# All eight Q/K pairs in one Strassen phase, and a rearranged attention pipeline (one-core decoder trunk)

## Chip, cores and metric

The kernel runs on one core of one Trainium2 chip. The metric is the device time of one execution in microseconds (us). A page of the profile and its trace come from one profiled execution. Engines: PE is the matrix engine, DVE the vector engine, ACT the scalar engine (activations), POOL is GpSimd, SP the engine whose queue starts most transfers.

## The reference, cut to what matters

Two layers on a sequence of 1024 positions with width 1024: first a short gated convolution, then dilated sliding-window attention, each followed by a SwiGLU feed-forward network; RMS norms stand between. All of it is float32. The change lies in the attention layer:

```python
BRANCHES = ((128, 1), (512, 4), (2048, 16))      # (window, dilation)

qkv = (h @ w_qkv).reshape(bsz, seq, 3, N_HEADS, HEAD_DIM)      # 16 heads of 64
q, k, v = qkv[:, :, 0], qkv[:, :, 1], qkv[:, :, 2]
for window, dilation in BRANCHES:
    o, l = dilated_branch(q, k, v, rel_bias, window, dilation)  # softmax over a strided band, and its log-sum
    outs.append(o); lses.append(l)
alpha = jax.nn.softmax(jnp.stack(lses, axis=0), axis=0)
o = jnp.sum(alpha[..., None] * jnp.stack(outs, axis=0), axis=0)
return o.reshape(bsz, seq, D_MODEL).astype(h.dtype) @ w_out
```

The kernel merges the three branches: one set of logits a head, one maximum, one sum.

## The kernel before

**Splitting.** Every float32 operand of a large product is split into a high part (rounded, written by ACT, line 145) and a low part (the rest, written by DVE, line 146), and a product is three matmuls: high by high, high by low, low by high. A weight that was loaded raw (line 159) is split a few products ahead of its use.

**Strassen units.** Most large products go through Winograd's form of Strassen: seven products instead of eight (class `Strassen`; its matmuls are lines 571 to 573, each of the seven takes four k blocks of three). `QueryKey` does this for the queries and keys of head pairs: a unit is one pair, its four output blocks are scaled, split and stored to DRAM (`emit`) a step at a time between later products. `QK_PAIRS` is the number of pairs it covers, seven of eight.

**Plain products.** `product` (lines 373 to 375) multiplies without Strassen. `projections` does pair 7 that way, inside attention. `value_tiles` makes the values of four heads at a time (lines 1517 to 1519, 256 wide), written to DRAM in `vdram`; the first such group is made before the first head.

**Attention slots.** The heads run in a software pipeline of slots, `slot(n)`. In slot n PE makes the scores of head n and applies the probabilities of head n-1 to the values. A slot has two loops of eight steps. In the first, each step takes one step of the scores (`scores`: matmuls, then DVE adds the bias and keeps the maximum, then POOL takes the maximum over partitions, line 1628) and one step of the softmax of the head before (`due`: a subtraction on DVE, line 1636, and an exponential on ACT, line 1637). In the second loop the value matmuls (`values`, line 1647) run. From slot `LAG` + 1 = 14 on, the softmax follows in the head's own slot, and the value matmuls stand in the first loop beside the scores.

**Fillers.** Between these, PE gets independent work from a generator `dense`: value groups 1 to 3, then pair 7's projections, then the first half of the output product (`out_product`, over the attended tiles of pairs 0 to 3). A step of it is mostly three 512-wide or six 256-wide matmuls; some steps are only an evacuation. `DENSE` holds the number of steps of each slot, by hand; 13 for most. In slots 1 to 12 ten of them lie in the first loop.

**Transfers.** In slot n the keys and queries of head n+1 are loaded (`load_kq`) and, for every second head, the values of a pair (`load_values`) into `vx`, of which there is one buffer. Its 16 blocks hold 64 columns of values of the first head, 64 of ones (they make the softmax's sum), and 64 of values of the second. Finished pairs are scaled and stored to `odram` (`attended`); those of pairs 0 to 3 are read back all four in slot 11 (`load_attended`) and split there for the output product.

**Banks.** All PSUM tiles are taken in turn from one pool of eight banks, so a bank is reused eight allocations later.

Of the kernel before, what the change touches and what calls it, by code (L numbers as in the profile page):

```python
# [10 lines left out]
F32 = mybir.dt.float32  # L11
F32R = mybir.dt.float32r
AF = mybir.ActivationFunctionType
# [7 lines left out]
H = 16  # L21
# [20 lines left out]
FFN_PAIRS, FFN_CHUNK = 9, 3  # L42
CONV_PAIRS, CONV_CHUNK, CO = 0, 1, 4
CONV, QK = "conv", "qk"
QK_PAIRS = 7
PAGES = 41
SOFT = 4
FIN0 = 2
# [1 line left out]
AO = 4  # L50
LAG = 13
EXTRA = (3, 7)
FILL = (("v", 0), ("v", 1), ("v", 2), ("v", 3), ("qk", 7))
DENSE = (13,) * 13 + (16, 13, 12, 11)
DEEP_ORDER = (1, 2, 5, 6, 7, 3, 4)


# [39 lines left out]
def view(t, off, dims):  # L97
    return bass.AP(tensor=t.tensor, offset=t.offset + off, ap=[t.ap[0]] + [list(d) for d in dims])
# [3 lines left out]
def trunk(ctx: ExitStack, tc: tile.TileContext, x, gains_in, cwi, ck, cwo, wqkv, wo, relb,  # L102
          wg, wu, wd, oneh, ident, out):
    nc = tc.nc
# [9 lines left out]
    scope = {}  # L114
# [20 lines left out]
    def split(src, dst=None, eng=nc.vector):  # L135

        w = src.shape[1]
        if dst is None:
            if w <= HALF:
                t = page("w", F32R)  # L140
                dst = t[:, :w], t[:, HALF:HALF + w]
            else:
                dst = page("w_hi", F32R)[:, :w], page("w_lo", F32R)[:, :w]
        hi, lo = dst
        nc.scalar.activation(hi, src, AF.Copy)  # L145
        eng.tensor_tensor(out=lo, in0=src, in1=hi, op=ALU.subtract)  # L146
        return hi, lo
# [1317 lines left out]
    def load_bias(h):  # L1465
        t = scope["pool"].tile([128, L1 + L2], F32, name="bias", tag="bias", bufs=2)
        base = tables.offset + h * G3
        nc.sync.dma_start(t[:, 0:L1], bass.AP(tensor=tables.tensor, offset=base, ap=[[1, 8], [A1, 16], [1, L1]]))
        nc.sync.dma_start(t[:, L1:L1 + L2], bass.AP(tensor=tables.tensor, offset=base + G0,
                                                    ap=[[1, 32], [A2, 4], [1, L2]]))  # L1470
        return t
# [8 lines left out]
    def attention(norm, qk):  # L1480
# [2 lines left out]
        qlo = [scope["pool"].tile([128, S], F32R, name=f"ql{a}") for a in range(2)]  # L1483
        for a in range(2):
            nc.gpsimd.memset(qlo[a][64 - 64 * a:128 - 64 * a].bitcast(F32), 0.0)
        vx = scope["pool"].tile([128, 16, 192], F32, name="vx", tag="vx", bufs=1)
        nc.vector.memset(vx[:, :, 64:128], 1.0)

        def projections(p):

# [37 lines left out]

        def load_values(p):
            src = vdram[p // 2]  # L1530
            for a in range(2):
                off = src.offset + p % 2 * 128 + a * 64
                dims = slice(128 * a, 128 * a + 64)
                nc.sync.dma_start(vx[:, 0:8, dims], bass.AP(src.tensor, off, [[256, 128], [128 * 256, 8], [1, 64]]))
                for h in range(2):
                    nc.sync.dma_start(vx[:, 8 + 4 * h:12 + 4 * h, dims],
                                        bass.AP(src.tensor, off + 512 * 256 * h, [[1024, 128], [256, 4], [1, 64]]))

        def load_kq(n):

# [99 lines left out]
        def values(p, a, st):  # L1640
            lf, lh, ld, lp = (st[n] for n in ("lf", "lh", "ld", "lp"))
            acc = [bank(), bank()]
            kd = [[128, 4], [1, 32]]
            b1 = [[32, 16], [1, 8]]

            def mm(ih, off, dims, u, rhs, first=False, last=False):
                nc.tensor.matmul(view(acc[ih], off, dims), vx[:, u, 64 * a:64 * a + 128], rhs,  # L1647
                                 start=first, stop=last)

            for ih in range(2):  # L1650
                for r4 in range(4):
                    mm(ih, r4 * 32, kd, 8 + r4, view(lf, ih * HALF + r4 * 32, kd), first=r4 == 0)
                    if r4 % 2:
                        yield
            for r4 in range(4):
                mm(1, r4 * 32, kd, 12 + r4, view(lh, r4 * 32, kd))
                if r4 % 2:
                    yield
            for j in range(8):
                off = (j % 4) * 8  # L1660
                mm(j // 4, off, b1, j, view(ld, blk(j), b1), last=False)
                if j:
                    mm(j // 4, off, b1, j - 1, view(lp, blk(j), b1), last=j % 4 == 3)
                yield
            o, z = st["o"], st["z"]
            n0 = slice(64 * a, 64 * a + 64)
            z0 = slice(64 - 64 * a, 128 - 64 * a)
            for ih in range(2):
                s = slice(ih * HALF, (ih + 1) * HALF)
                nc.scalar.activation(z[n0, s], acc[ih][z0], AF.Ln)  # L1670
                nc.scalar.activation(o[n0, s], acc[ih][n0], AF.Copy)
            yield

        def finish(p):
# [39 lines left out]
        put_off, ending, due = [], [], [iter(())]  # L1714
        OZ, acts = {}, {}

        def slot(n, dense, ndense, late=0, hook=iter(())):

            def other(k):
                for _ in range(k):  # L1720
                    next(dense, None)

            p, a = divmod(n, 2)
            if n < H:
                new = dict(bias=bias.pop(n))
                sc = scores(p, a, new)
            else:
                sc = iter(())
            if n + 1 < H:
                load_kq(n + 1)  # L1730
                bias[n + 1] = load_bias(n + 1)
            if n:
                q, b = divmod(n - 1, 2)
                if b == 0:
                    OZ[q] = page("o"), page("z")
                old = live.pop(n - 1)
                old.update(o=OZ[q][0], z=OZ[q][1])
                pv = values(q, b, old)
            else:
                pv = iter(())  # L1740
            extra = later = iter(())
            lagged = n <= LAG
            if n + 1 < H:
                later = classes(n + 1)
            if lagged and a and p:
                ending.append(finish(p - 1))
            used = 0
            if lagged:
                for i in range(8):
                    next(due[0], None)  # L1750
                    next(sc, None)
                    k = 1 + (i in EXTRA and n < LAG) if n else i % 2
                    other(k)
                    used += k
                    if a and ending and i == 4:
                        run(ending.pop())
                run(sc)
            else:
                if a == 0 and not late:
                    other(1)  # L1760
                    used += 1
                for i in range(8):
                    next(sc, None)
                    next(pv, None)
                    next(pv, None)
                    if i >= late and i % 2 == 0:
                        other(1)
                        used += 1
                run(sc)
                run(pv)  # L1770
                if a == 0:
                    extra = finish(p - 1)
                if a == 0 and n < H:
                    load_values(p)
            left = max(ndense - used, 0)
            for i in range(8):
                next(pv, None)
                next(pv, None)
                if i == (2 if n > LAG + 1 else 5):
                    attended()  # L1780
                if not lagged and (i < FIN0 or i > SOFT):
                    next(extra, None)
                if i in (1, 2):
                    next(later, None)
                if i < 4:
                    next(hook, None)
                if i == (3 if lagged else SOFT) and n < H:
                    live[n] = new
                    due[0] = softmax(new)
                    if n >= LAG:  # L1790
                        run(due[0])
                other(left * (i + 1) // 8 - left * i // 8)
            run(pv)
            run(extra)

        def load_attended(ps):
            raw = {p: page("oin") for p in ps}
            for p in ps:
                nc.sync.dma_start(raw[p], odram[p])
            return raw  # L1800
# [27 lines left out]
        done, first = {}, {}  # L1828

        def fill():  # L1830
            for kind, g in FILL[1:]:
                if kind == "qk":
# [3 lines left out]
                        yield from value_tiles(g, j)  # L1836
            yield from out_product(0, range(AO), first)

        def halves():
            for q, t in done.items():  # L1840
                first[q] = split(t)
                yield

        dense = fill()
        for n in range(H):
            if n == LAG - 2:
                done.update(load_attended(range(AO)))
            hook = halves() if n == LAG - 2 else iter(())
            slot(n, dense, DENSE[n], 3 if n == H - 2 else 0, hook)
            run(hook)  # L1850
        acts.update(split_attended(load_attended(range(AO, 7))))
        ensure(ahead_ao)
# [44 lines left out]
    with tc.tile_pool(name="first", bufs=1) as scope["pool"]:  # L1897
# [5 lines left out]
        qk = QueryKey(norm)  # L1903
# [132 lines left out]
```

## Time and profile before

| | |
|---|---|
| time, median of 3 runs | 2103.48 us (2102.67 to 2103.56) |
| the profiled execution | 2105.08 us, span of its instructions 2103.3 us |
| granted PE clock in it | 0.998 |
| DMA over the span | 300.70 MB, 143 GB/s; 48236 of 141495 packets under 512 bytes |

The slots start at (first score matmul): slot 0 at 1123.8 us, slot 4 at 1186.8, slot 9 at 1272.8, slot 12 at 1325.6, slot 13 at 1344.5, slot 14 at 1365.4, slot 15 at 1385.1; the value matmuls of head 15, in slot 16, start at 1403.9. In a profile row of a group stand its busy time, the mean of one instruction in nanoseconds, and the idle time just before them with what ended it; in a row of the timeline stand the start, the duration, the engine, the line and the tiles. In a row of windows stand each engine's busy time in that stretch, the granted PE clock, and the share and rate of the DMA engines.

### The profile page before, as it was taken

To read this page: it belongs to the slowest core of one execution; us is meant where nothing else is said; L and a number is where in the kernel's file an instruction comes from. 1 tells how busy PE (TensorE), PEld (TensorE's weight loads), DVE (VectorE), ACT (ScalarE), POOL (GpSimd) and SP (SyncE) were. 2 spreads that over 40 slices of the span, in tenths; PEclk is the share of its full clock that TensorE was granted. 3 is DMA by queue.
4 is the path that set the end of the run, shared out by engine and by line. 5 is a ranking of instruction groups with operands and counts; after the bars stand their busy time and mean duration, and the time that the engine had idled before them with its cause. 6 is when DMAs were issued, how large, how long until landed. Compare 5 with 4: busy or idle time off the path is not lost. (4 is left out here: it accounts for less than half of the span.)

```text
span 2103.3 us, 30766 instructions
## 1 busy us (share of the span) xinstructions
PE 2083.1 (99%) x10990; PEld 1792.2 (85%) x10990; DVE 1746.1 (83%) x3264; ACT 1013.7 (48%) x1852; POOL 240.0 (11%) x336
## 2 busy tenths in 40 slices
PE   9999999999999999999999999999999999999998
PEld 7788888888888888887789999988788888888887
DVE  8898769988888788968984778987998888888886
ACT  7433427444444454445553566555544434456433
POOL 1000000110101010010223232211011001001000
PEclk9999999999999999999999999999999999999999
DMA  7322643233333467452658788955223323368432
GB/s 216 100 96 71 230 135 76 101 105 111 102 105 110 145 201 208 133 159 65 232 201 209 161 202 210 250 165 154 71 87 108 107 99 113 110 194 245 158 96 80
DMA packets 141495, 300.70 MB, mean 143 GB/s; under 512 B 48236, under 2 KB 54462, under 8 KB 141344
## 3 DMA queue, kind: packets, MB, share of 16 engines
q1 hardware_dynamic: 107488, 201.94, 32.4%
q0 software_dynamic: 26224, 82.11, 12.6%
q10 hardware_dynamic: 7632, 14.70, 1.9%
q8 instruction: 87, 1.43, 0.3%
q14 instruction: 64, 0.52, 0.1%
HBM read 208.42 MB, written 82.93 MB: 139 GB/s over the span
## 5 line engine op out<-in xcount | busy, mean ns | idle before, releaser
L573 PE MATMUL bank<-b,w 128*128 128x512 f32 x1980 | 772.5, 390 | 5.4 <-DVE w L146 5.2
L571 PE MATMUL bank<-b,w 128*128 128x512 f32 x1980 | 772.3, 390 | 2.3 <-ACT w L145 1.1
L572 PE MATMUL bank<-b,w 128*128 128x512 f32 x1980 | 771.9, 390 | 0.6 <-DVE b L882 0.6
L573 PEld LDWEIGHTS bank<-b,w 128*128 128x128 f32 x1980 | 372.0, 188 | 87.5 <-DVE w L146 10.5
L571 PEld LDWEIGHTS bank<-b,w 128*128 128x128 f32 x1980 | 372.3, 188 | 80.3 <-ACT w L145 1.9
L572 PEld LDWEIGHTS bank<-b,w 128*128 128x128 f32 x1980 | 372.3, 188 | 76.6 <-DVE b L882 1.2
L145 ACT ACTIVATE w<-combo 128x512 fp32r<-128x512 f32 (+2 forms) x492 | 251.5, 541 | 238.9 <-DVE combo L193 219.7
L146 DVE TENSOR_TENSOR w<-combo,w 128x512 fp32r<-128x512 f32 (+2 forms) x492 | 279.8, 582 | 37.8 <-ACT w L145 37.0
L577 ACT ACTIVATE part<-bank 128x512 f32<-128x512 f32 x189 | 112.5, 595 | 383.9 <-PE bank L573 378.7
L146 DVE TENSOR_TENSOR w<-raw,w 128x512 fp32r<-128x512 f32 (+2 forms) x345 | 194.4, 585 | 36.5 <-ACT w L145 36.5
L581 DVE TENSOR_TENSOR part<-part,bank 128x256 f32<-128x256 f32 (+1 forms) x369 | 173.1, 499 | 31.9 <-PE bank L573 17.3
L145 ACT ACTIVATE w<-raw 128x512 fp32r<-128x512 f32 (+2 forms) x345 | 168.5, 531 | 47.8 <-PE bank L573 12.2
L373 PE MATMUL bank<-w_hi,w 128*128 128x512 f32 (+1 forms) x400 | 151.0, 378 | 0.1
L375 PE MATMUL bank<-w_hi,w 128*128 128x512 f32 (+1 forms) x400 | 149.3, 373 | 0.7 <-DVE w L146 0.7
L374 PE MATMUL bank<-w_lo,w 128*128 128x512 f32 (+1 forms) x400 | 149.0, 373 | 0.0
L801 DVE TENSOR_TENSOR x<-x,bank 128x512 f32<-128x512 f32 x136 | 92.9, 683 | 28.7 <-PE bank L573 28.7
L492 DVE TENSOR_TENSOR x<-x,bank 128x512 f32<-128x512 f32 (+1 forms) x104 | 66.7, 644 | 59.8 <-PE bank L375 58.9
L193 DVE TENSOR_TENSOR combo<-raw 128x512 f32<-128x512 f32 (+1 forms) x174 | 112.6, 648 | 0.0
L375 PEld LDWEIGHTS bank<-w_hi,w 128*128 128x128 f32 x400 | 75.3, 188 | 14.8 <-DVE w L146 1.6
L564 DVE TENSOR_TENSOR b<-hin,b 128x512 fp32r<-128x512 f32 x126 | 79.5, 686 | 9.4 <-ACT b L563 9.4
L373 PEld LDWEIGHTS bank<-w_hi,w 128*128 128x128 f32 x400 | 75.5, 189 | 12.3 <-ACT w L145 0.5
L374 PEld LDWEIGHTS bank<-w_lo,w 128*128 128x128 f32 x400 | 75.5, 189 | 11.9
(234 smaller groups left out, 3377.0 us busy)
## 6 DMA issues: line engine op xcount, KB each, us to landing
hin<-part SPq DMA_DIRECT2D x126, 256.0 KB
raw<-in_ffn_w_gate SPq DMA_DIRECT2D x44, 512.0 KB
raw<-in_ffn_w_up SPq DMA_DIRECT2D x44, 512.0 KB
part<-sum POOLq DMA_DIRECT2D x72, 256.0 KB, 2.3
raw<-in_ffn_w_down SPq DMA_DIRECT2D x48, 384.0 KB
raw<-in_attn_w_qkv SPq DMA_DIRECT2D x27, 512.0 KB
raw<-in_conv_w_in SPq DMA_DIRECT2D x24, 512.0 KB
part<-part POOLq DMA_DIRECT2D x36, 256.0 KB, 2.6
```

What stands on the lines that cost most here:

```text
L145: nc.scalar.activation(hi, src, AF.Copy)
L146: eng.tensor_tensor(out=lo, in0=src, in1=hi, op=ALU.subtract)
L193: eng.tensor_tensor(out=c, in0=a, in1=b, op=op)
L373: nc.tensor.matmul(b, whi[:, a], ahi[:, s], start=first, stop=False)
L374: nc.tensor.matmul(b, whi[:, a], alo[:, s], start=False, stop=False)
L375: nc.tensor.matmul(b, wlo[:, a], ahi[:, s], start=False, stop=last)
L571: nc.tensor.matmul(b, hi[:, a], bhi, start=start and k == 0, stop=False, skip_group_check=True)
L572: nc.tensor.matmul(b, hi[:, a], blo, start=False, stop=False, skip_group_check=True)
L573: nc.tensor.matmul(b, lo[:, a], bhi, start=False, stop=k == n - 1, skip_group_check=True)
L577: nc.scalar.activation(t, b, AF.Copy)
L581: nc.vector.tensor_tensor(out=t, in0=t, in1=b, op=ALU.add)
L801: nc.vector.tensor_tensor(out=X[n][:, half(h)], in0=X[n][:, half(h)], in1=b, op=ALU.add)
```

## The change

- `QK_PAIRS` goes from 7 to 8: pair 7 becomes one more Strassen unit, and its `projections` leave the fillers.
- `DENSE` is rewritten for the fewer filler steps, 184 in all where there were 221: 11 in slots 0 to 8, 10 in slots 9 and 10, 11 in 11 and 12, then 14, 10, 10 and 9.
- In the first loop of a slot the score step comes before the softmax step, and the softmax starts one step later.
- The blocks of `vx` begin with the ones, so that the values of a pair's two heads are adjacent; a pair is loaded in three DMAs with pieces of 512 bytes instead of six with pieces of 256. The sum and the output of a head change places in the accumulators.
- The attended tiles of pairs 0 and 1 are loaded and split in slot 9, those of pairs 2 and 3 in slot 10, instead of all four in slot 11.

```diff
-QK_PAIRS = 7
+QK_PAIRS = 8
...
-FILL = (("v", 0), ("v", 1), ("v", 2), ("v", 3), ("qk", 7))
-DENSE = (13,) * 13 + (16, 13, 12, 11)
+FILL = (("v", 0), ("v", 1), ("v", 2), ("v", 3))
+OIN = LAG - 3
+DENSE = (11,) * 9 + (10, 10) + (11, 11, 14, 10, 10, 9)
...
-        vx = scope["pool"].tile([128, 16, 192], F32, name="vx", tag="vx", bufs=1)
-        nc.vector.memset(vx[:, :, 64:128], 1.0)
+        vx = scope["pool"].tile([128, 16 * 192 + 64], F32, name="vx", tag="vx", bufs=1)
+        nc.vector.memset(view(vx, 0, [[192, 17], [1, 64]]), 1.0)
...
-            for a in range(2):
-                off = src.offset + p % 2 * 128 + a * 64
-                dims = slice(128 * a, 128 * a + 64)
-                nc.sync.dma_start(vx[:, 0:8, dims], bass.AP(src.tensor, off, [[256, 128], [128 * 256, 8], [1, 64]]))
-                for h in range(2):
-                    nc.sync.dma_start(vx[:, 8 + 4 * h:12 + 4 * h, dims],
-                                        bass.AP(src.tensor, off + 512 * 256 * h, [[1024, 128], [256, 4], [1, 64]]))
+            off = src.offset + p % 2 * 128
+            nc.sync.dma_start(view(vx, 64, [[192, 8], [1, 128]]),
+                              bass.AP(src.tensor, off, [[256, 128], [128 * 256, 8], [1, 128]]))
+            for h in range(2):
+                nc.sync.dma_start(view(vx, (8 + 4 * h) * 192 + 64, [[192, 4], [1, 128]]),
+                                  bass.AP(src.tensor, off + 512 * 256 * h, [[1024, 128], [256, 4], [1, 128]]))
...
-                nc.tensor.matmul(view(acc[ih], off, dims), vx[:, u, 64 * a:64 * a + 128], rhs,
+                nc.tensor.matmul(view(acc[ih], off, dims), vx[:, u * 192 + 128 * a:u * 192 + 128 * a + 128], rhs,
                                  start=first, stop=last)
...
-                nc.scalar.activation(z[n0, s], acc[ih][z0], AF.Ln)
-                nc.scalar.activation(o[n0, s], acc[ih][n0], AF.Copy)
+                nc.scalar.activation(z[n0, s], acc[ih][n0], AF.Ln)
+                nc.scalar.activation(o[n0, s], acc[ih][o0], AF.Copy)
...
-        def slot(n, dense, ndense, late=0, hook=iter(())):
+        def slot(n, dense, ndense, late=0, hook=iter(()), ps=()):
...
                 bias[n + 1] = load_bias(n + 1)
+            done.update(load_attended(ps))
...
                 for i in range(8):
-                    next(due[0], None)
                     next(sc, None)
+                    if i > 0:
+                        next(due[0], None)
                     k = 1 + (i in EXTRA and n < LAG) if n else i % 2
...
         for n in range(H):
-            if n == LAG - 2:
-                done.update(load_attended(range(AO)))
-            hook = halves() if n == LAG - 2 else iter(())
-            slot(n, dense, DENSE[n], 3 if n == H - 2 else 0, hook)
+            ps = {OIN - 1: (0, 1), OIN: (2, 3)}.get(n, ())
+            hook = halves(ps)
+            slot(n, dense, DENSE[n], 3 if n == H - 2 else 0, hook, ps)
             run(hook)
```

More of the change, by code (lines that the diff above doesn't have):

```diff
@@ L1666, in values @@
             n0 = slice(64 * a, 64 * a + 64)
-            z0 = slice(64 - 64 * a, 128 - 64 * a)
+            o0 = slice(64 - 64 * a, 128 - 64 * a)
             for ih in range(2):
                 s = slice(ih * HALF, (ih + 1) * HALF)
-                nc.scalar.activation(z[n0, s], acc[ih][z0], AF.Ln)
-                nc.scalar.activation(o[n0, s], acc[ih][n0], AF.Copy)
+                nc.scalar.activation(z[n0, s], acc[ih][n0], AF.Ln)
+                nc.scalar.activation(o[n0, s], acc[ih][o0], AF.Copy)
             yield
@@ L1837, in fill, with halves @@
             yield from out_product(0, range(AO), first)
-        def halves():
-            for q, t in done.items():
-                first[q] = split(t)
+        def halves(ps):
+            for q in ps:
+                first[q] = split(done.pop(q))
                 yield
```

## The prediction

> **What bounds the kernel now.** I read the page's busy shares first, then busy time by stage (the windows), then the matmuls in order of time, then who waits for whom, and last the chain score – maximum – exponential – values head by head.
>
> ```profile
> PE 2083.1 (99%) x10990; PEld 1792.2 (85%) x10990; DVE 1746.1 (83%) x3264; ACT 1013.7 (48%) x1852; POOL 240.0 (11%) x336
> ```
>
> ```profile
> core 0: us, PE busy (x) PEld busy (x) DVE busy (x) ACT busy (x) POOL busy (x), PEclk, DMA share, GB/s
> 1080.00:1100.00 20.00, 20.00 (x90) 16.57 (x89) 17.23 (x26) 10.66 (x17) 4.88 (x9) 1.00 0.50 179
> 1186.80:1272.80 86.00, 86.00 (x745) 86.00 (x745) 65.21 (x121) 52.41 (x75) 26.13 (x21) 1.00 0.69 168
> 1272.80:1325.60 52.80, 52.80 (x367) 48.62 (x366) 48.02 (x81) 33.51 (x45) 18.59 (x15) 1.00 1.06 258
> 1365.40:1385.10 19.70, 18.94 (x127) 17.20 (x126) 16.52 (x32) 12.87 (x19) 3.78 (x2) 1.00 0.53 154
> ```
>
> The rows are the end of the Q and K phase, slots 4 to 8, slots 9 to 11 and slot 14. TensorE (PE) has no gap in the first three; the only attention stage with a visible one is slot 14 (0.76 us). So matmuls set the time, and a matmul saved is time saved, as long as VectorE (DVE) and the head-to-head chain keep up. DVE is at 65.21/86.0 = 76% in slots 4 to 8, but at 48.02/52.8 = 91% in slots 9 to 11: room there is small.
>
> A busy mean is not a matmul's price, because matmuls overlap. The price is the distance between starts:
>
> ```profile
> 1089.63 0.39 PE L573 MATMUL bank<-b,w 128*128 128x512 f32 x1
> ...
> 1090.99 0.39 PE L573 MATMUL bank<-b,w 128*128 128x512 f32 x1
> ```
>
> ```profile
> 1278.40 0.40 PE L373 MATMUL bank<-b,w_hi 128*128 128x512 f32 x1
> ...
> 1279.10 0.28 PE L1574 MATMUL bank<-qa,ka 128*128 128x256 f32 x1
> ```
>
> ```profile
> 1262.02 0.28 PE L1517 MATMUL bank<-w_hi,b 128*128 128x256 f32 x1
> 1262.14 0.28 PE L1518 MATMUL bank<-w_lo,b 128*128 128x256 f32 x1
> ```
>
> First fence: six steps in 1.36 us, 0.227 us for a 512-wide matmul in the Q/K phase, though each lasts 0.39. Second: three such matmuls as a filler among the scores, 0.233 each. Third: 0.12 for a 256-wide matmul of a value filler.
>
> **The change, part by part.**
>
> *Pair 7 moves.* As filler it is 2 parts x 2 halves x 8 k x 3 = 96 matmuls: 96 x 0.227 to 0.233 = 21.8 to 22.4 us out of attention. In the phase it is one more unit of 7 products x 4 k x 3 = 84 matmuls: 84 x 0.227 = 19.1 us more. Net -2.7 to -3.3; I take **-3.0**. The added unit's splits, sums, part sums and outputs lie beside its 19.1 us of matmuls; the row of 1080 to 1100 shows the same mix with DVE at 17.23 of 20 and PE full, so I cost it at nothing (uncovered, it costs what a split comes late).
>
> *Fewer fillers in slots 0 to 12.* A slot there takes 86.0/5 = 17.2 us with 13 fillers. A value filler averages 24/5 matmuls x 0.12 = 0.58 us, so 11 fillers give about 16.05 us, 10 (slots 9, 10) 15.5. DVE needs 65.21/5 = 13.0 us of it, and beside that it waits:
>
> ```profile
> DVE lf L1636 <- POOL mb L1628: 32.1, 12, 3.5
> ```
>
> 2.7 us a time, 12 times, DVE stands at the first subtraction until GpSimd's maximum is there, with the next head's logits queued behind. 13.0 + 2.7 = 15.7 of 16.05 would be tight. With the logits first, the four additions of the first two score steps fall into that wait:
>
> ```profile
> 1273.96 1.23 DVE L1636 TENSOR_TENSOR lf<-lf,mb 128x1024 f32<-128x1024 f32 x1 [3.46 <-POOL mb L1628]
> 1275.11 0.75 DVE L1585 TENSOR_TENSOR lf<-bank,bias 128x256 f32<-128x256 f32 x2
> ...
> 1281.23 0.42 DVE L1611 TENSOR_TENSOR ld<-bank,bias 128x256 f32<-128x256 f32 x1
> ...
> 1283.09 0.42 DVE L1611 TENSOR_TENSOR ld<-bank,bias 128x256 f32<-128x256 f32 x1
> ```
>
> ```profile
> 1281.35 0.63 ACT L1637 ACTIVATE lp<-lp 128x512 f32<-128x512 f32 x1 [0.74 <-DVE lp L1636]
> ```
>
> ```profile
> 1286.62 0.39 PE L1647 MATMUL bank<-lp,vx 128*128 128x128 f32 x2
> ```
>
> Price of the order: the first subtraction, 1.2 us into slot 9 (start 1272.8), now stands behind the second score step's additions, which I place 2.6 us in (two score steps and a filler of 0.6 to 0.7 on PE, then 0.7 on DVE). From there to the end of the last one it was 1281.23 - 1273.96 = 7.3 us; two pairs of additions (1.3) leave that stretch, the group of 1281.23 to 1283.09 (1.9) and one more pair (0.7) enter it: 8.6. With 0.6 for the last exponential that makes 11.8 us, where it was 9.2 (1281.98). Its first reader is the value matmul four steps after the row at 1286.62, at about 1287.9, 15.1 in; without the one filler that lies before it in the second loop (0.7), and with value fillers, some 14.0. Slack falls from about 5.9 to 2.2 us: positive, so **0** for these slots, bounds -0.3 and +7 (below, the first rival).
>
> ```profile
> L146 DVE TENSOR_TENSOR w_lo<-oin,w_hi 128x1024 fp32r<-128x1024 f32 x4 | 6.3, 1638 | 0.0
> ```
>
> *Attended tiles two and two.* Their four splits (6.3 us of DVE in all, 1.64 each, where the 1024-wide subtraction at 1273.96 takes 1.23) go from slot 11 to slots 9 and 10, behind the head's last maximum, in the same wait. Slots 9 and 10 lose pair 7's outputs, so DVE has 13.0 + 2 x 1.6 = 16.2 against 15.5: a lag of under 1 us a slot, inside the 2.2. **0**.
>
> *Values in 512-byte pieces.* 4096 pieces of 256 bytes a pair become 2048, six DMAs three. But the first head's values now need all of the pair's load, and no part of it can start before the pair before is done.
>
> ```profile
> 1273.36 0.47 SPq L1534 DMA_DIRECT2D vx<-vdram  x1
> ...
> 1276.36 1.84 SPq L1536 DMA_DIRECT2D vx<-vdram  x2
> ```
>
> ```profile
> 1282.80 1.95 PE L1647 MATMUL bank<-lf,vx 128*128 128x128 f32 x16
> ```
>
> ```profile
> DMA packets 52757, 60.84 MB, mean 203 GB/s; under 512 B 36576, under 2 KB 40672, under 8 KB 52729
> ...
> odram<-o POOLq DMA_DIRECT2D x7, 512.0 KB, 5.8
> ```
>
> Before, six issues are out at 1278.2, 4.6 us ahead of the first reader, at a DMA share of 1.06. Three issues take about half the 4.8 us and leave some 7. **0**, bound +3 a pair in slots 9 and 11. I take the lower bound, since most packets of the stage are under 512 bytes, and those of the values halve. [...]
>
> *Slots 13 to 16.* Fillers go from 16, 13, 12, 11 to 14, 10, 10, 9. A filler is 3 x 0.227 = 0.68 us. Here a head's values follow its own softmax directly:
>
> ```profile
> 1369.09 0.33 PE L1574 MATMUL bank<-qa,kca 128*128 128x128 f32 x1 [0.76 <-ACT o L1671]
> ...
> 1385.56 1.05 PE L1647 MATMUL bank<-lf,vx 128*128 128x128 f32 x8
> ```
>
> ```profile
> 1382.84 1.06 ACT L1637 ACTIVATE lf<-lf 128x1024 f32<-128x1024 f32 x1 [0.86 <-DVE lf L1636]
> ...
> 1402.83 1.06 ACT L1637 ACTIVATE lf<-lf 128x1024 f32<-128x1024 f32 x1 [3.97 <-DVE lf L1636]
> ```
>
> ```profile
> 1403.52 0.39 PE L375 MATMUL bank<-w_hi,w 128*128 128x512 f32 x1
> 1403.95 1.16 PE L1647 MATMUL bank<-lf,vx 128*128 128x128 f32 x8
> ```
>
> Slot 15: the exponential ends at 1383.90, its reader starts at 1385.56, slack 1.66; three fillers fewer are 2.04: a new wait of **+0.4**. Slot 16: ends at 1403.89, PE was free at 1403.75, slack none; two fillers fewer: **+1.3**. Slot 14: the 0.76 us is the third score step waiting for the bank of the first half of head 12, eight allocations back. With two fillers fewer one filler bank less lies between, so this score step gets another bank, and the fourth asks for that one about when it is free: **-0.5** (bounds -0.8 and +1.0, if it still waits while PE arrives 1.4 us earlier).
>
> Sum: -3.0 + 0 + 0 + 0 + 0.4 + 1.3 - 0.5 = **-1.8 us**. The profiled execution (span 2103.3, time 2105.08) would become 2103.3; against the median of 2103.48, 0.08% lower, **2101.7**.
>
> **The rivals.**
>
> *First, slower: DVE becomes the clock of slots 1 to 12.* A 1024-wide weight split inside the first loop costs 1.2 us and, since it now stands right behind a subtraction, waits for that exponential and its own copy on ScalarE (1.06 in the rows above for each 1024-wide pass). That is 3.3 against 2.2 of slack: 1.1 us in each of four slots; slots 9 to 12 with attended splits and the output product's additions 0.75 each: +7.4. It decides once DVE's work plus its waits pass the slot's 15.5 to 16.05. Time 2101.7 + 7.4 = **2109.1**. For it: 91% in slots 9 to 11, and both edits shorten the slot. Against: pair 7's own DVE work leaves just those slots.
>
> *Second: loads are late in slots 9 to 11.* Attended tiles 2 and 3 are loaded one slot after being written, the values all at once, at DMA share 1.06; ScalarE stands at the split with the next head's key copies queued behind it, and PE at the next scores. Two waits of 2 us: 2101.7 + 4 = **2105.7**. Against: the store lands in a median of 5.8 us of a 15.5 us slot. [...]
>
> *Third: no wait is left.* -3.3 and the 0.76 + 0.2 of waiting gone: -4.2, **2099.3**. For it only that DVE, freed of pair 7, might pass maxima on earlier; the slot 16 chain speaks against.
>
> *Fourth: the moved unit does not run at full rate* because its splits come late, and the saving of 3.0 is lost: **2104.7**. The 1080 to 1100 row speaks against.
>
> **How the numbers follow.** Forecast 0.48, first rival 0.19, second 0.13, third 0.14, fourth 0.06. 0.2% is 4.2 us, about what a measurement here can tell from no change. Faster by more takes most of the third: 0.13. Slower by more takes the first and some of the second: 0.21. Within: 0.66. The range leaves out half of the first and the lowest of the third: 2099.0 to 2108.0.
>
> **What would show it.** 84 more matmuls on L571 to L573, 96 fewer on L373 to L375. The Q/K phase some 19 us longer without new gaps; 2.7 us of waiting for the maximum mostly gone; slots of 16 us with PE full. PE waits of about 1.5 us ahead of the values in slot 16 and 0.4 in slot 15. Waits of PE for L1637 or L1585 in slots 1 to 12 would mean the first rival, of ScalarE's splits for attended tiles or of PE for values the second.

## The result and the profile after

The changed kernel takes 2123.38 us (median of 4 runs, 2122.09 to 2124.17), the kernel before 2103.40 us in the same comparison (2102.67 to 2103.56): a ratio of 1.0095, 95% interval 1.0078 to 1.0113. It is 20 us slower; the forecast was 1.8 us faster, with a range up to 2108.0. The profiled execution took 2123.89 us with a span of 2122.1, 18.8 more than before. Lines of the new kernel are one higher than before up to the values (the split is L146 and L147, the product L374 to L376); the score and softmax lines keep their numbers.

The matmuls changed as the diff says. From the page after, the busy line and one group:

```profile
PE 2086.6 (98%) x10978; PEld 1794.5 (85%) x10978; DVE 1754.5 (83%) x3276; ACT 1016.9 (48%) x1860; POOL 238.2 (11%) x336
...
L574 PE MATMUL bank<-b,w 128*128 128x512 f32 x2008 | 783.4, 390 | 5.4 <-DVE w L147 5.1
```

12 matmuls fewer in all. Each of the three Strassen lines has 2008 where it had 1980, 84 more; the 96 of pair 7's projections (`bank<-b,w_hi` and `bank<-b,w_lo`, 32 on each of L373 to L375) are gone. Where the time is, by the start of the first score matmul of a slot:

| stage | before | after | difference |
|---|---|---|---|
| all up to slot 0 | 1123.8 | 1144.4 | +20.6 |
| slots 0 to 3 | 63.0 | 60.2 | -2.8 |
| slots 4 to 8 | 86.0 | 86.4 | +0.4 |
| slots 9 to 11 | 52.8 | 54.9 | +2.1 |
| slots 12 and 13 | 39.8 | 36.9 | -2.9 |
| slot 14 | 19.7 | 19.1 | -0.6 |
| slot 15 to the values of head 15 | 18.8 | 21.6 | +2.8 |
| the rest | 699.4 | 698.6 | -0.8 |

21.8 us of filler matmuls left attention, and from slot 0 to the values of head 15 it became 1.0 us shorter (only 2 of the 37 steps lie behind that). In slots 4 to 11, where some 11 us of fillers went (18 steps of 0.6), it became 2.5 us longer. The windows of after, for the stages shown of before:

```profile
1080.00:1111.00 31.00, 29.75 (x132) 24.31 (x131) 24.66 (x39) 13.42 (x25) 7.44 (x14) 1.00 0.42 141
...
1204.60:1291.00 86.40, 83.23 (x697) 83.04 (x696) 63.12 (x119) 49.70 (x71) 25.39 (x17) 0.96 0.58 155
1291.00:1345.90 54.90, 50.60 (x387) 48.32 (x386) 46.55 (x79) 32.54 (x45) 13.33 (x13) 0.97 0.88 247
1382.80:1401.90 19.10, 17.13 (x118) 15.54 (x117) 15.78 (x30) 12.33 (x18) 3.78 (x2) 1.00 0.40 118
```

Before, PE had no gap in the first three rows and the clock was 1.00. Now PE idles 1.3, 3.2, 4.3 and 2.0 us, and two rows have a granted clock under 1. For whom PE waits, in the waits of after (total, times, longest); none of these but the second (5.2 before) and the fourth (1.1) was above 0.4 us before:

```profile
PE bank L1647 <- ACT lp L1637: 6.9, 4, 3.2
PE bank L574 <- DVE w L147: 5.1, 6, 1.9
PE bank L1647 <- ACT lf L1637: 4.9, 3, 2.6
PE bank L572 <- ACT w L146: 2.3, 2, 1.6
PE bank L572 <- ACT part L578: 1.7, 2, 1.3
...
PE bank L1574 <- ACT kca L1558: 1.0, 2, 0.6
PE bank L1574 <- DVE x L493: 0.9, 1, 0.9
```

L1647 with lp is the end of a head's softmax, in slots 2, 6, 10 and 11 (1.0, 3.2, 1.1 and 1.6 us); L1647 with lf is its beginning, in slots 14, 15 and 16 (1.0, 1.3 and 2.6 us). The longest wait, in slot 6 (which starts at 1236.2), read back from PE through ACT to DVE in the timeline:

```profile
1252.07 0.79 PE L1647 MATMUL bank<-lp,vx 128*128 128x128 f32 x2 [3.17 <-ACT lp L1637]
```

```profile
1246.77 1.05 ACT L146 ACTIVATE w_hi<-raw 128x1024 fp32r<-128x1024 f32 x1
1251.49 0.52 ACT L1637 ACTIVATE lp<-lp 128x384 f32<-128x384 f32 x1 [3.68 <-DVE lp L1636]
```

```profile
1237.86 1.23 DVE L147 TENSOR_TENSOR w_lo<-raw,w_hi 128x1024 fp32r<-128x1024 f32 x1 [3.67 <-ACT w_hi L146]
1239.00 1.41 DVE L1585 TENSOR_TENSOR lf<-bank,bias 128x256 f32<-128x256 f32 x4
1240.33 1.22 DVE L1636 TENSOR_TENSOR lf<-lf,mb 128x1024 f32<-128x1024 f32 x1
...
1247.85 1.22 DVE L147 TENSOR_TENSOR w_lo<-raw,w_hi 128x1024 fp32r<-128x1024 f32 x1 [2.57 <-ACT w_hi L146]
...
1250.85 0.55 DVE L1636 TENSOR_TENSOR lp<-lp,mb 128x384 f32<-128x384 f32 x1
```

The first weight split of the slot keeps DVE standing until ACT has copied the high half; behind it stand the four first logit additions, and only behind those the first subtraction, 4.1 us into the slot. The second split stands in the middle of the softmax, 2.57 us of waiting and 1.22 of work. The last subtractions come after it, ACT's exponential after them, PE after that.

### The profile page after: what moved, and what is told of

It is laid out like the page before. It is cut to its first block, busy times and chain, and to the rows that moved or that the text cites. A ratio compares the mean times of both kernels' runs of the same rounds, so it can differ in the third digit from the quotient of the medians.

```text
span 2122.1 us, 30718 instructions
## 1 busy us (share of the span) xinstructions
PE 2086.6 (98%) x10978; PEld 1794.5 (85%) x10978; DVE 1754.5 (83%) x3276; ACT 1016.9 (48%) x1860; POOL 238.2 (11%) x336
## 2 busy tenths in 40 slices
DMA packets 124727, 300.70 MB, mean 142 GB/s; under 512 B 15084, under 2 KB 37694, under 8 KB 124576
## 5 line engine op out<-in xcount | busy, mean ns | idle before, releaser
L574 PE MATMUL bank<-b,w 128*128 128x512 f32 x2008 | 783.4, 390 | 5.4 <-DVE w L147 5.1
L572 PE MATMUL bank<-b,w 128*128 128x512 f32 x2008 | 783.2, 390 | 4.3 <-ACT w L146 2.3
L573 PE MATMUL bank<-b,w 128*128 128x512 f32 x2008 | 782.8, 390 | 0.3 <-DVE b L883 0.3
L574 PEld LDWEIGHTS bank<-b,w 128*128 128x128 f32 x2008 | 377.3, 188 | 88.9 <-DVE w L147 10.5
L572 PEld LDWEIGHTS bank<-b,w 128*128 128x128 f32 x2008 | 377.5, 188 | 83.3 <-ACT w L146 3.1
L573 PEld LDWEIGHTS bank<-b,w 128*128 128x128 f32 x2008 | 377.4, 188 | 77.5 <-DVE b L883 1.2
L146 ACT ACTIVATE w<-combo 128x512 fp32r<-128x512 f32 (+2 forms) x496 | 253.9, 542 | 239.5 <-DVE combo L194 220.8
L147 DVE TENSOR_TENSOR w<-combo,w 128x512 fp32r<-128x512 f32 (+2 forms) x496 | 282.6, 583 | 39.4 <-ACT w L146 38.6
L578 ACT ACTIVATE part<-bank 128x512 f32<-128x512 f32 x192 | 114.3, 595 | 382.8 <-PE bank L574 380.8
L147 DVE TENSOR_TENSOR w<-raw,w 128x512 fp32r<-128x512 f32 (+2 forms) x348 | 194.6, 580 | 46.1 <-ACT w L146 46.1
L146 ACT ACTIVATE w<-raw 128x512 fp32r<-128x512 f32 (+2 forms) x348 | 170.5, 531 | 56.5 <-PE bank L574 21.5
L374 PE MATMUL bank<-w_hi,w 128*128 128x512 f32 (+1 forms) x400 | 150.9, 377 | 0.1
L376 PE MATMUL bank<-w_hi,w 128*128 128x512 f32 (+1 forms) x400 | 149.3, 373 | 0.7 <-DVE w L147 0.7
L375 PE MATMUL bank<-w_lo,w 128*128 128x512 f32 (+1 forms) x400 | 149.0, 373 | 0.0
L376 PEld LDWEIGHTS bank<-w_hi,w 128*128 128x128 f32 x400 | 75.3, 188 | 14.8 <-DVE w L147 1.6
L374 PEld LDWEIGHTS bank<-w_hi,w 128*128 128x128 f32 x400 | 75.4, 189 | 12.1 <-ACT w L146 0.5
L375 PEld LDWEIGHTS bank<-w_lo,w 128*128 128x128 f32 x400 | 75.5, 189 | 11.7
```

The source lines that it names most:

```text
L374: nc.tensor.matmul(b, whi[:, a], ahi[:, s], start=first, stop=False)
L375: nc.tensor.matmul(b, whi[:, a], alo[:, s], start=False, stop=False)
L376: nc.tensor.matmul(b, wlo[:, a], ahi[:, s], start=False, stop=last)
L572: nc.tensor.matmul(b, hi[:, a], bhi, start=start and k == 0, stop=False, skip_group_check=True)
L573: nc.tensor.matmul(b, hi[:, a], blo, start=False, stop=False, skip_group_check=True)
L574: nc.tensor.matmul(b, lo[:, a], bhi, start=False, stop=k == n - 1, skip_group_check=True)
```

## The experiments

Unless a sentence says otherwise, ratios are against the kernel before, which took 2103.32 to 2103.59 us (medians) on the chips that were used.

**The order of the loop, undone and done alone.** Edit to after, and the reverse edit to before:

```diff
                 for i in range(8):
+                    next(due[0], None)
                     next(sc, None)
-                    if i > 0:
-                        next(due[0], None)
```

> The changed kernel with the softmax step put back ahead of the score step; all else as changed. Theory A (the order): logits first makes the last exponentials of a head late, so the waits of PE for the lp exponentials (6.9 us in four places) and their after-effects go: about 2123 - 11 = 2112 us or less, PE waiting for L1637 only in slots 13 to 16. Theory B (the cover): 11 or 10 fillers are too few for VectorE whatever the order; with the old order the 2.7 us wait for the maximum comes back in each slot: 2123 us or more.

> The kernel before with logits ahead of subtractions, nothing else. Theory A: with 13 fillers a slot there is some 1.2 us more slack a slot, so it costs less than in the changed kernel, but some slots with a weight split wait: 2106 to 2112 us. Theory B: the order itself is harmless or helps: 2102.5 to 2103.5 us.

After with the old order: 2112.75 us, ratio 1.0042 (1.0025 to 1.0059), so 10.6 us of the 20 come back. Before with the new order: 2112.27 us, 1.0042 (1.0027 to 1.0056): 8.7 us lost with every filler in place. The longest waits of PE from 1090 us on, of the first:

```profile
PE bank L1647 <- ACT lf L1637: 4.9, 3, 2.6
PE bank L572 <- ACT part L578: 1.3, 1, 1.3
```

and of the second:

```profile
PE bank L1647 <- ACT lp L1637: 5.4, 4, 2.3
```

The waits for lp are absent with the old order and are there without any other edit: they belong to the order. The waits for lf and for L578 stay when it is undone: they come from something else in the change (the runs below part the tail and the phase).

**The order with the softmax from the first step on** (before, `next(sc)` ahead of `next(due[0])`, without the skipped step):

> The kernel before with the score step ahead of the softmax step, but the softmax starting at the first step, not the second: half of the change in order. If the loss is the latency of the last exponentials (each step of delay costs what PE then waits), this loses clearly less than the full change of order (8.7 us): 2104 to 2108 us. If any change of order loses by blocking, about the same 2112.

2106.91 us, 1.0015 (1.0006 to 1.0025): 3.6 us instead of 8.7. The softmax is delayed by one score step instead of two, and the loss is under half: the work is the same and only its latency differs.

**The splits' low halves issued two steps later** (after; then the best of the kernels with eight pairs below; then, as a control, before with its values in 512-byte pieces):

```diff
-        eng.tensor_tensor(out=lo, in0=src, in1=hi, op=ALU.subtract)
+        low = lambda: eng.tensor_tensor(out=lo, in0=src, in1=hi, op=ALU.subtract)
+        if later_on[0]:
+            lows.append(low)
+        else:
+            low()
...
+                    if k == 5:
+                        flush_lows()
```

> The changed kernel, but of the weight splits made among the value fillers VectorE's half (the low part) is issued two filler steps after ScalarE's half, not right behind it. If VectorE standing at these splits (3.7 and 2.6 us in slot 6) is what makes the last exponentials late, the waits in the slots with splits (some 8 us around slots 2, 5, 6, 9 and 10) mostly go: 2115 to 2119 us. If it is the order alone, whatever stands in the queue, 2122 to 2124.

> The kernel before with 512-byte values and the low halves issued later. PE has no wait in slots 1 to 12 to lose, so no difference: 2103.4 us within 1. A control for the two runs beside it: a difference would mean that the later low halves do something else.

After: 2115.18 us, 1.005 (1.0033 to 1.0066), 8.2 less than without the edit. The control: 2103.66, 1.0 (0.9991 to 1.001); in the kernel before, where PE has no gap from slot 0 to slot 11, the edit is worth nothing. A window of the first (its profiled execution took 2118.75 us, the slowest of four), the longest wait of PE that is left in slots 0 to 12, and a row of DVE ahead of it, then the same row in after:

```profile
1144.40:1300.00 155.60, 155.60 (x1347) 155.60 (x1345) 124.59 (x234) 91.11 (x129) 47.62 (x37) 1.00 0.76 192
```

```profile
PE bank L1661 <- ACT lp L1651: 4.0, 1, 4.0
```

```profile
1333.07 0.69 DVE L503 TENSOR_TENSOR x<-x,bank 128x512 f32<-128x512 f32 x1 [4.79 <-DMA x<-spill]
```

```profile
1340.84 0.69 DVE L493 TENSOR_TENSOR x<-x,bank 128x512 f32<-128x512 f32 x1 [3.15 <-DMA x<-spill]
```

In this kernel (L1661 is the values, L1651 the exponential) PE has no gap from slot 0 to 1300 us: the waits in slots 2 and 6 are gone, with the order still in place, and DVE's waits for a high half in slots 0 to 11 fell from 9.2 to 2.5 us. So in these slots DVE standing at a split for its ScalarE half is what the order cannot bear. The 4.0 us wait is in slot 11 and has another cause. There the output product begins; its first addition stands on DVE for a load of x, with the last subtraction of the softmax queued behind it. In after the same load holds DVE for 3.15 us, and the 1.6 us wait of slot 11 follows. The kernel before has no such wait of DVE in attention.

**Attended tiles two and two, alone** (before, `load_attended` of pairs 0 and 1 in slot 9, 2 and 3 in slot 10):

> The kernel before with only the attended tiles two and two, in slots 9 and 10. Theories A and B: VectorE does the same work one or two slots earlier while pair 7's outputs still lie there; 2103 to 2106 us. Rival C (loads late in slots 9 to 11): ScalarE waits at the splits, the key copies come late, PE waits 2 us or more in slots 10 and 11: 2106 to 2110.

2108.69 us, 1.0026 (1.0016 to 1.0037), 5.1 us lost. The longest waits of PE in attention, and the rows of ACT in front of the two of them:

```profile
PE bank L1575 <- ACT kca L1559: 3.9, 2, 2.4
```

```profile
1287.63 1.06 ACT L146 ACTIVATE w_hi<-oin 128x1024 fp32r<-128x1024 f32 x1 [6.80 <-PE bank L1648]
...
1308.23 0.63 ACT L1146 ACTIVATE kq_hi<-kq 128x512 fp32r<-128x512 f32 x1 [2.33 <-DVE kq L1141]
```

PE's score matmuls wait for the key copies on ACT at the start of slots 10 and 11. In the first (1.5 us) the copies are queued behind the split of an attended tile, which stands 6.80 us, by its releaser until the slot's value matmuls are through; whether it lacked a buffer or the tile was late is open. In the second (2.4 us) they are queued behind a copy for pair 7 that waits 2.33 us for DVE, and behind another such split. DVE itself had stood 1.75 us for the landing of the finished pair's store.

**Values in 512-byte pieces, alone** (before with the new `vx` and its three DMAs):

> The kernel before with only the values in 512-byte pieces (ones first, three loads a pair). Theories A and B: no wait of PE for values, 2103.4 us within 1 us. Rival C (the one load of both heads is late, since none of it can start before the pair before is done): PE waits for vx, some us more, 2105 to 2110.

2103.39 us, 1.0 (0.999 to 1.0009): nothing, either way.

**The short tail, alone.** All the fillers of before, but slots 13 to 16 with after's 14, 10, 10, 9 (the rest go to slot 12):

```diff
-DENSE = (13,) * 13 + (16, 13, 12, 11)
+DENSE = (13,) * 12 + (22, 14, 10, 10, 9)
```

> The kernel before with the fillers of slots 13 to 16 cut to those of the changed kernel (14, 10, 10, 9) and the nine put into slot 12 (22), so that VectorE comes to slot 13 without a lag and no matmul is saved. By the prediction's step for slots 13 to 16 the shorter slots cost 0.4 + 1.3 - 0.5 = 1.2 us: 2104.0 to 2105.5. If the 6.5 us of waits there in the changed kernel (1.2 before) come from the fillers alone and not from a lag brought along, about 5 us: 2107.5 to 2109.5.

2107.07 us, 1.0017 (1.0008 to 1.0026), 3.5 us lost. The waits of PE in attention:

```profile
PE bank L1647 <- ACT lf L1637: 3.0, 2, 1.7
PE bank L1574 <- ACT o L1671: 0.6, 1, 0.6
```

In slot 15 the subtraction starts 0.9 us after its maximum came (1381.73 + 3.23 = 1384.96), because a split stands ahead of it:

```profile
1381.73 3.23 POOL L1628 PARTITION_ALL_REDUCE mb<-m  x1 [7.39 <-DVE m L1625]
```

```profile
1385.29 0.69 DVE L146 TENSOR_TENSOR w<-raw,w 128x512 fp32r<-128x512 f32 x1 [2.11 <-ACT w L145]
1385.90 1.22 DVE L1636 TENSOR_TENSOR lf<-lf,mb 128x1024 f32<-128x1024 f32 x1
```

**Eight pairs with the fillers placed for the tail.** The old order, all four attended tiles in slot 11, ten fillers in slots 0 to 11, and before's 16, 13, 12 in 13 to 15:

```diff
-DENSE = (11,) * 9 + (10, 10) + (11, 11, 14, 10, 10, 9)
+DENSE = (10,) * 12 + (13, 16, 13, 12, 10)
```

Then the same with the Q/K phase's last operand (x12) loaded and split one unit later, and the same with the attended tiles two and two; then the late operand with deferred low halves.

> Eight pairs in the phase, 512-byte values, the old order; the attended tiles again all four in slot 11, and the fillers 10 in slots 0 to 11, then 13, 16, 13, 12, 10, so that slots 13 to 16 have what they had in the kernel before (one less in 16). If the loss left in the run with the old order comes from the two-and-two loads (about 3 us) and from the short slots 13 to 16 (6.5 us of waits where the kernel before has 1.2), both go: the 2.7 us of matmuls are gained, the wait of 1.4 us in the phase stays: 2101 to 2103 us. If 10 fillers are too few for VectorE (rival B), PE waits in slots 1 to 12 for L1637 or for banks: 2106 us or more.

> As the run with ten a slot, and the Q/K phase loads and splits the last operand (x12, four pages) one unit later, after product (6, 7) instead of (5, 7). If PE's wait at the end of the phase (1.4 us, for a ScalarE copy behind a weight split that waits for a page) comes from pages held by that operand, it goes: 1.4 us less than the run with ten a slot. If the page was short for another reason, no difference within 0.5 us.

> As the run with ten a slot, but the attended tiles two and two in slots 9 and 10. If it is these loads that make ScalarE's key copies late, 2 to 5 us above the run with ten a slot, with PE waiting for L1558 (key copies) at the start of slots 10 and 11. If the place of the loads doesn't matter, the two are equal within 1 us.

> The run with ten a slot, old order and the late x12, with the low halves issued two steps later as well. With 10 fillers the slots without a split just run through (15.6 us); those with splits lose 1.1, 3.3 and some 7 us. If VectorE's standing at the splits is the cause, most of the first two and part of the third go: 2104 to 2109 us; if it is the splits' work itself (1.2 us each), 2111 to 2113.

2113.68 us (1.0047, 1.0031 to 1.0064); 2112.41 (1.0041, 1.0026 to 1.0056); 2112.35 (1.0043, 1.0028 to 1.0058); 2108.48 (1.0023, 1.0014 to 1.0033). The first was to come to 2101 to 2103 us if the tiles and the short tail made the whole remaining loss. It missed that by over 10 us and fell in the other case, too few fillers: the tail's waits for lf went, and some 6 us of others came in slots 0 to 12, with the old order in place. Two attended tiles in each of two slots made no loss here (1.3 us less). In the run with x12 later the 1.3 us wait for L578 at the end of the phase is absent from the waits. The last is the best with eight pairs that was run, 4.9 us over the kernel before; deferring the low halves is worth 3.9 us to it. Its longer waits in attention are 2.0 us for low halves of the output product's operands and 1.9 us for key copies.

No kernel with eight pairs or with the new order beats the kernel before. Whether some placement of 184 fillers would is open.

## Why the prediction was wrong

**Pair 7 moves: right.** At 0.227 us from start to start, which the rows of after have too, 12 matmuls fewer are 2.7 us, the lower end of 2.7 to 3.3. The "cost at nothing" of the added unit failed by 1.4 us:

```profile
1092.88 0.63 ACT L146 ACTIVATE w<-raw 128x512 fp32r<-128x512 f32 x1 [4.58 <-PE bank L574]
1093.41 0.58 ACT L578 ACTIVATE part<-bank 128x512 f32<-128x512 f32 x1
```

```profile
1094.05 0.50 PE L572 MATMUL bank<-b,w 128*128 128x512 f32 x1 [1.25 <-ACT part L578]
```

The split of a weight waits 4.58 us until PE is through earlier matmuls, and ACT's evacuation of a bank is queued behind it; the row of 1080 to 1100 before does not show what happens at the seam between two units. Loading another operand, x12, one unit later removed the wait; that the split lacked a page which x12 held is inferred from that. The fourth rival, with the whole 3.0 lost, was too dear; its mechanism, a late split, was right.

**Fewer fillers and the order, costed at 0: the step that failed.** Its arithmetic held where no split falls in the loop. Slot 9 starts at 1291.0:

```profile
1291.65 1.42 DVE L1585 TENSOR_TENSOR lf<-bank,bias 128x256 f32<-128x256 f32 x4 [3.98 <-PE bank L1575]
1292.99 1.22 DVE L1636 TENSOR_TENSOR lf<-lf,mb 128x1024 f32<-128x1024 f32 x1
```

```profile
1300.35 0.52 ACT L1637 ACTIVATE lp<-lp 128x384 f32<-128x384 f32 x1 [1.27 <-DVE lp L1636]
...
1302.09 0.61 ACT L1637 ACTIVATE lp<-lp 128x512 f32<-128x512 f32 x1
```

```profile
1303.54 0.39 PE L1647 MATMUL bank<-lp,vx 128*128 128x128 f32 x2
```

The last exponential ends at 1302.70, 11.7 us in, where 11.8 was forecast, and PE passes through that head's values without a wait. What was wrong is what happens to the idle time of DVE. The first subtraction was to use the wait for the maximum for logit additions. The waits of DVE over slots 0 to 11, before and after:

```profile
DVE lf L1636 <- POOL mb L1628: 29.0, 10, 3.5
```

```profile
DVE lf L1585 <- PE bank L1575: 28.8, 13, 4.8
```

The wait for the maximum is gone, as forecast, and as much idle time stands now at the first logit addition, which waits for PE's score matmuls with the softmax queued behind it. In slot 9 the maximum is there 0.1 us into the slot:

```profile
1287.85 3.22 POOL L1628 PARTITION_ALL_REDUCE mb<-m  x1 [11.70 <-DVE m L1625]
```

DVE stands for PE until 1291.65, and comes to the subtraction 1.9 us after the maximum (1291.07 to 1292.99). So no idle time of DVE was filled, while the chain against PE had lost its cover: by the forecast's own sum, 5.9 us of slack were 2.2.

The first rival named the mechanism, a weight split standing for ScalarE inside the loop, and had 0.19. It counted one split a slot, 3.3 against 2.2 of slack, 1.1 lost.

```profile
1180.38 1.23 DVE L147 TENSOR_TENSOR w_lo<-raw,w_hi 128x1024 fp32r<-128x1024 f32 x1 [2.07 <-ACT w_hi L146]
```

That is slot 2 of after: one split, 2.07 + 1.23 = 3.3, and PE waits 1.0. In slot 6 two fall in: the first subtraction comes 4.1 us in instead of 2.0 (2.1 late), and the second split takes 2.57 + 1.22, 5.9 in all. PE waits there for the first of the two lp exponentials, which in slot 9 ends 2.7 us ahead of its reader (1300.87 to 1303.54): 5.9 less 2.7 is 3.2, and 3.2 was waited. That the rival's 7.4 us in total stands so near the 6.9 of waits for lp is partly luck. Weight splits made 4.2 of these, in two slots where it counted four; slot 10's 1.1 stands behind the attended tiles' splits, which put its first subtraction 5.4 us in, and slot 11's 1.6 behind the load of x, which no rival had.

The step that failed is the choice of 0 between -0.3 and +7 for the new order with fewer fillers: the one-split sum already came to 1.1 us a slot and was set aside for a rival's price. In its place the runs showed 8.7 us for the order alone and 10.6 gained by undoing it in the changed kernel; and with the old order and ten fillers a slot, PE still waits some 6 us in slots 0 to 12.

**Attended tiles, costed at 0: wrong alone, lost among the rest in the change.** Alone 5.1 us, with two waits of together 3.9 us, the second rival's 2 x 2 us in size and place. Its mechanism, key copies queued behind a standing split, is there in the first; in the second they stand mainly behind a copy that waits for DVE, and that a load was late is not shown. In after the key copies cost PE 1.0 us, and the splits the waits of slot 10 above. The prediction counted the splits as a lag of DVE, under 1 us a slot; it did not follow the key copies behind them in ACT's order.

**512-byte values at 0: right**, inside its bound of +3: in after the packets under 512 bytes fell from 48236 to 15084, and with the values in 512-byte pieces alone the time was 2103.39 us, ratio 1.0. The forecast took its lower bound because fewer short packets were left; no run shows a price for them.

**Slots 13 to 16, +1.2: too small.** Alone the new tail costs 3.5 us. In slot 15 1.3 us of waiting stands against the forecast 0.4, since the chain itself came 0.9 later by the split ahead of its subtraction; the forecast moved PE's reader forward and held the DVE steps where they were. In slot 16 1.7 stands against 1.3, and the 0.5 that slot 14 was to gain did not come (0.6 of waiting alone and 0.9 in after, where 0.8 was). In after the waits for lf are 4.9 us, and in slot 16 the same happens one step earlier: the last steps of the maximum stand behind an addition and a split of the output product.

```profile
1415.10 0.68 DVE L493 TENSOR_TENSOR x<-x,bank 128x512 f32<-128x512 f32 x1
1415.70 0.69 DVE L147 TENSOR_TENSOR w<-raw,w 128x512 fp32r<-128x512 f32 x1
1416.30 0.68 DVE L1624 TENSOR_TENSOR m<-m,ld 128x512 f32<-128x512 f32 x1
...
1421.13 1.23 DVE L1636 TENSOR_TENSOR lf<-lf,mb 128x1024 f32<-128x1024 f32 x1 [3.42 <-POOL mb L1628]
```

**The sum.** Matmuls -2.7; the seam in the phase +1.3 by its wait; waits in attention 6.9 + 4.9 + 1.0 + 0.9 and 0.6 for another exponential, less 0.8 before, +13.5; time at half clock (last section) +4.3: +16.4 of the 18.8 us between the spans. The other 2.4 us are not assigned to rows. The reading behind the forecast, that matmuls set the time and one saved is time saved, held in the kernel before, with 13 fillers a slot, and in no run with 10 or 11. The fillers were also what covered the softmax: with 21.8 us of them gone, the loop of DVE, ScalarE and PE set the time in the slots with splits. What is shown by single edits is the order's share (8.7 alone, 10.6 when undone), the tail's (3.5) and the tiles' (5.1 alone); these overlap and don't add up to 20. What the fewer fillers cost by themselves was not measured alone.

## What to carry to other kernels

Before removing independent work from a pipeline, follow the dependent chain of a stage with its worst case in it, here two splits in one slot and not the mean: taking away work that fills a wait saves only the part of it that goes beyond the wait (here 21.8 us of fillers went, and from slot 0 to the values of head 15 it became 1.0 us shorter). An instruction that is moved ahead in an in-order queue brings its own wait with it (here 28.8 us of DVE at the first logit additions, where 29.0 at the first subtractions had been), so ask what it waits for, and not only into which gap its duration fits. An operation that goes over two engines can be issued in two places, so that the second engine doesn't stand for the first; here that was worth 8.2 us in the changed kernel, and nothing in the kernel before, where PE had no gap from slot 0 to slot 11.

## What the runs showed of the hardware

Some waits of PE cost more than their length here. Stretches of after, behind the long wait in slot 6 and later, and then behind the waits in slots 10 and 16:

```profile
1252.00:1257.50 5.50, 5.43 (x25) 5.43 (x26) 2.48 (x6) 4.21 (x7) 2.73 (x1) 0.50 0.09 20
1258.00:1262.00 4.00, 4.00 (x36) 4.00 (x36) 2.33 (x5) 1.18 (x2) 0.00 (x0) 1.00 0.66 185
```

```profile
1322.70:1326.00 3.30, 3.30 (x15) 3.30 (x16) 3.27 (x7) 2.92 (x5) 0.54 (x1) 0.51 0.50 120
1423.50:1427.00 3.50, 3.50 (x28) 3.37 (x29) 2.26 (x4) 3.34 (x6) 0.00 (x0) 1.00 0.02 5
```

For 5.5 us after the wait in slot 6 the granted clock is 0.50, and 25 matmuls run where at the rate of the next row (9 a us) they take 2.8: by this estimate 2.7 us on top of 3.2. From 1322.7 to 1326.0, after waits of 0.6 and 1.1 us, another 1.6 us goes (15 matmuls at 9 a us take 1.7 of 3.3). After the 2.6 us in slot 16 the clock stays at 1.00. Behind a wait of the same 2.6 us at the same place, in after with the old order, it is 0.50; and in the kernel before with the new order it is 0.52 behind the 2.3 us wait:

```profile
1412.50:1415.50 3.00, 3.00 (x13) 2.71 (x12) 1.67 (x4) 3.00 (x5) 0.00 (x0) 0.50 0.02 5
```

```profile
1168.30:1171.60 3.30, 3.30 (x19) 3.30 (x18) 1.34 (x3) 3.26 (x6) 1.73 (x1) 0.52 0.86 139
```

So here waits of 2.3 us and less were followed by a halved clock, and of two waits of 2.6 us one was and one was not; the length alone doesn't decide, and what does is not shown. The sums of the prediction count a wait at its length and have no time at half clock; in after that time adds 4.3 us to the waits, by the two estimates above (2.7 and 1.6).
